# Output projection of a two-branch attention layer: 28 of 64 pairs of weight row tiles as seven block products of sums

## The chip, the cores and the metric

The kernel runs on one core of one Trainium2 chip. The metric is the device time in microseconds (us), the median of three runs; lower is better.

## What is computed

One decoder layer on 256 tokens (S) of 4096 channels (D), all in float32:

```python
proj = rmsnorm(x, g_pre) @ w_in          # 18336 columns, split into the parts below
o_a = causal_dense_attention(...) * silu(gate_a)      # branch A, 16 heads, 2048 wide
o_b = indexed_sparse_attention(...) * silu(gate_b)    # branch B, 16 heads, 2048 wide
merged = sigmoid(merge_a) * (o_a @ p_a) + sigmoid(merge_b) * (o_b @ p_b)
out = x + merged @ w_o                   # w_o is 4096 x 4096
```

The change concerns the last line, `merged @ w_o`, and what leads into it.

## The kernel before

Every float32 matrix product is made of three products of split operands: each operand is a high part (rounded to the type that TensorE takes at full rate) and a low part (the rest), and `mm3` issues high x high, low x high and high x low (L96, L97, L98) into one PSUM accumulator. The stationary side of a product is a 128 x 128 block of the transposed activations, the moving side 128 x 512 of a weight.

**The weight stream.** `run_streams` walks over a list, `plan`, of units. A unit is two weight row tiles (256 rows) by 512 columns: one DMA of 512 KB into `raw`, one cast on ScalarE (ACT) into `hi` (L218), one subtraction on VectorE (DVE) into `lo` (L226), and on TensorE (PE) 2 row tiles x 2 token tiles x 3 = 12 products of 128 x 512. `hi` and `lo` have three buffers and are issued two units ahead, `raw` has four and its DMA is issued six units ahead. All engines work through their instructions in the order in which the program issued them, each engine on its own. PE holds no instruction back for another engine except through semaphores.

**Background work.** All other work is written as generators. `tick`, called once per unit, lets them go on as far as a credit for DVE and ACT allows; `drain` runs them to their end at once. What a generator issues stands in the engines' order where it was issued.

**The last part.** For each of 8 chunks of 512 columns the stream has 16 units of `w_in` for each of the two sigmoid gates, 8 units of `p_a` and 8 of `p_b`; then `merged` (the tile `sa`, products and sums on DVE) is transposed on PE, and for chunks 0 to 6 stored to DRAM (`mt_d`). When the product with `p_a` of chunk 7 begins, `pre_last` starts seven background loads (`load_mt`): each reads one stored chunk into a tile `mts` (two buffers, DMA issued by GpSimd, POOL) and splits it, one ACT cast and one DVE subtraction of 128 x 1024, into `mh` and `ml` (tiles `h0`.., `l0`..), the stationary side of the output projection. Chunk 7 is transposed and split without going through DRAM. The projection itself is 8 chunks of 512 columns x 16 units of `w_o`, in the same stream; `final` adds `x` and stores.

Of the kernel before, what the change touches and what calls it, by code (L numbers as in the profile page):

```python
# [37 lines left out]
def kernel(ctx: ExitStack, tc: tile.TileContext, x, positions, g_pre, w_in, g_q_lat,  # L38
# [18 lines left out]
    class Meter:  # L57
        """An engine whose instructions are charged, by their size, to the background's share of its time."""
# [75 lines left out]
    def release(what):  # L134
        held[what] -= 1
# [40 lines left out]
    plan = []  # L176

# [9 lines left out]
    def run_streams():  # L187
# [43 lines left out]
        # the first pair of weight tiles is split tile by tile, on both engines, to start the products early  # L231
# [30 lines left out]
        for i, (spec, u) in enumerate(units):  # L262
            stat, w, segs, done, pre, each = spec
            if u == 0:
# [7 lines left out]
                if spec is units[-1][0]:  # L272
                    accs[id(spec)][0][1] = flat(ps_at.tile([P, 2, S], F32, name="at"))
# [8 lines left out]
            for kk in range(2):  # L282
# [14 lines left out]
                elif i == n - 1:  # L297
                    continue
                else:
                    for m in range(2):  # L300
                        ms = slice(m * P, (m + 1) * P)
                        mm3(accm[m][:, :wd], xh[:, ms], xl[:, ms], his[i][:, kk, :wd], los[i][:, kk, :wd],
                            k == 0, k == nk - 1)
# [4 lines left out]
            if i == n - 1:  # L308
                for m in range(2):
                    ms = slice(m * P, (m + 1) * P)  # L310
                    for kk in range(2):
                        k = 2 * u + kk
                        xh, xl = stat[1](k)
                        mm3(accm[m], xh[:, ms], xl[:, ms], his[i][:, kk, :], los[i][:, kk, :], False, kk == 1)
                    final_rows(accm[m], m)
                continue
            his[i] = los[i] = None
            if k == nk - 1:
                active.insert(0, done(acc))

# [1 line left out]
    # products of zeros keep the tensor engine busy until the first data is there, so that its clock is up by then  # L322
    zeros = cp.tile([P, 512], BF16, name="zeros")
# [9 lines left out]
    zero1 = cp.tile([P, 1], F32, name="zero1")  # L333
    dve.memset(zero1, 0.0)
    nhalf = cp.tile([P, 16], F32, name="nhalf")
    dve.memset(nhalf, -0.5)
    warm = cp.tile([P, 1], F32, name="warm")
# [7 lines left out]
    cst_sb = cp.tile([P, 33], F32, name="cst_sb")  # L345
    gT = cp.tile([P, 48], F32, name="gT")
    grot = cp.tile([P, 2, 64], F32, name="grot")
    posb = cp.tile([P, S], F32, name="posb")
    posp = cp.tile([P, 2], F32, name="posp")
    cm = cp.tile([P, 2, S], F32, name="cm")  # L350
    rope_q = cp.tile([P, 2, 2, 2, 64], F32, name="rope_q")
    rope_k = cp.tile([P, 2, 2, 64], F32, name="rope_k")
    r = cp.tile([P, 2], F32, name="r")
    krr = cp.tile([P, 2, 64], F32, name="krr")
    sskr = cp.tile([P, 2], F32, name="sskr")
    ssx = cp.tile([P, 2, 8], F32, name="ssx")
# [3 lines left out]
    wk_stack = ExitStack()  # L360
# [187 lines left out]
    def prep_rope():  # L548
# [21 lines left out]
        # rope_*[.., 0, ..]: multiplies x; rope_*[.., 1, ..]: multiplies x with its halves swapped  # L570
# [138 lines left out]
    def softmax_pv(s, nmx, sign, vh, vl, o_dst):  # L709
        """exp(sign * s + nmx), where nmx is minus the maximum of sign * s."""  # L710
# [310 lines left out]
    # each pair's two short streams lie within a long one, whose time its attention takes  # L1021
# [10 lines left out]
    M = {"go": [None, None], "mh": [], "ml": []}  # L1032

    def open_p():
        A["stack"].close()
        wk_stack.close()
        pp = M["pp"] = ctx.enter_context(tc.tile_pool(name="ppool", bufs=1))
        for br in range(2):
            M["go"][br] = (pp.tile([P, NH, S], F32R, name=f"goh{br}"), pp.tile([P, NH, S], F32R, name=f"gol{br}"))
# [42 lines left out]

    def load_mt(c):
# [5 lines left out]
        split(M["mh"][c], M["ml"][c], raw)  # L1089
# [6 lines left out]

    def done_pb(j):
        def done(acc):
            sa, sb = M["sa"], M["sb"]
            dve.tensor_tensor(sb, acc, sb, op=ALU.mult)  # L1100
            release("acc")
            dve.tensor_tensor(sa, sa, sb, op=ALU.add)
            if j < 7:
                spawn(store_merged(sa, j), ready=None)
                yield
            else:
                yield
                yield
                for kp in range(2):
                    tr = transpose_merged(sa, kp)  # L1110
                    split(flat(M["mh"][7][:, 2 * kp:2 * kp + 2, :]), flat(M["ml"][7][:, 2 * kp:2 * kp + 2, :]), tr)
                    yield
        return done

    def pre_last():
# [3 lines left out]
        for c in range(7):  # L1119
            spawn(load_mt(c), space=2)  # L1120

    for j in range(8):
# [4 lines left out]
        stream(stat_go(1), p_b, [(c0, 512)], done_pb(j))  # L1127

# [1 line left out]
    stat_m = (KT, lambda k: (M["mh"][k // 4][:, k % 4, :], M["ml"][k // 4][:, k % 4, :]))  # L1130

    def final(j):
        c0 = 512 * j

        def pre():
            xr = M["xr", j] = M["pp"].tile([P, 2, 512], F32, name="sb" if j % 2 else "xr")
            nc.gpsimd.dma_start(xr, xf[:, c0:c0 + 512].rearrange("(m p) c -> p m c", p=P))

        def done(acc):
            xr = M["xr", j]  # L1140
            dve.tensor_tensor(xr, acc, xr, op=ALU.add)
            release("acc")
            nc.gpsimd.dma_start(of[:, c0:c0 + 512].rearrange("(m p) c -> p m c", p=P), xr)
            yield

        stream(stat_m, w_o, [(c0, 512)], done, pre=pre)

    for j in range(8):
        final(j)

    def final_rows(acc, m):
        """The last chunk's rows of one token tile, in two halves so that the first is under way early."""
        xr = M["xr", 7]
        for q in range(2):
            cs = slice(256 * q, 256 * q + 256)
            dve.tensor_tensor(xr[:, m, cs], acc[:, cs], xr[:, m, cs], op=ALU.add)
            nc.sync.dma_start(of[m * P:(m + 1) * P, 7 * 512 + 256 * q:7 * 512 + 256 * q + 256], xr[:, m, cs])
# [3 lines left out]
    drain()  # L1161

# [42 lines left out]
```

## Time and profile before

| | |
|---|---|
| median of three runs | 2530.6 us (2530.31 to 2530.65) |
| span of the profiled execution, first to last instruction | 2528.1 us |
| PE busy | 2521.0 us (100% of the span) |
| DVE busy | 1392.0 us (55%) |
| ACT busy | 1221.6 us (48%) |
| POOL busy | 88.6 us (4%) |
| granted TensorE clock, mean | 1.000 |

The span leaves out what lies before the first and after the last instruction; against the median of the runs that is 2.5 us. A profiled PE matmul's own duration overlaps the next one's; its price is the distance from its start to the next start.

### The profile page before, as it was taken

What the parts mean: (1) busy time and instruction counts of PE and PEld (TensorE: products, weight loads), DVE (VectorE), ACT (ScalarE), POOL (GpSimd) and SP (SyncE); (2) the same over time, 40 slices, a digit from 0 to 9 for tenths busy, and PEclk for the clock granted to TensorE, in tenths of its full rate; (3) what the DMA queues carried; (4) which work ended last, traced back from release to release, by engine and by line L of the source; (5) the groups of instructions that cost most, each with busy time, mean ns of one, the idle gap of its engine ahead of it and who ended that gap; (6) DMA issues with size and microseconds to landing.
All of it is one profiled execution on the core that took longest, in us unless ns stands there. A gap on an engine that the chain in (4) does not pass through costs nothing.

```text
span 2528.1 us, 31510 instructions
## 1 busy us (share of the span) xinstructions
PE 2521.0 (100%) x12054; PEld 2108.7 (83%) x12054; DVE 1392.0 (55%) x1689; ACT 1221.6 (48%) x1646; POOL 88.6 (4%) x119
## 2 busy tenths in 40 slices
PE   9999999999999999999999999999999999999999
PEld 7988888888888888888888888888888888888887
DVE  5666696655666655655544444444444444644444
ACT  6555545555665555554444444444444434433333
POOL 2000000000000000000000000000000000000000
PEclk9999999999999999999999999999999999999999
DMA  7655565555555565557665656565656566666664
GB/s 245 185 168 166 160 187 161 167 183 175 181 185 177 186 183 186 185 179 244 214 199 195 197 196 198 194 198 193 199 192 200 192 216 205 237 226 214 217 217 158
DMA packets 259878, 490.46 MB, mean 194 GB/s; under 512 B 24660, under 2 KB 38096, under 8 KB 259728
## 3 DMA queue, kind: packets, MB, share of 16 engines
q1 hardware_dynamic: 251104, 460.38, 57.3%
q0 software_dynamic: 8576, 28.06, 3.2%
q8 instruction: 94, 1.54, 0.2%
q14 instruction: 56, 0.46, 0.0%
q10 hardware_dynamic: 48, 0.02, 0.0%
HBM read 474.24 MB, written 14.16 MB: 193 GB/s over the span
## 4 chain that ended last, share of the span: by engine, by line
PE 99%; DMA 0%; SPq 0%; issue 0%; DVE 0%; ACT 0%; DVEq 0%
PE acc L96 31%; PE acc L97 31%; PE acc L98 31%; PE tr L119 2%; PE at L96 1%; PE at L98 1%; PE at L97 1%; PE tr L618 0%; DMA raw<-in_w_in 0%; PE at L656 0%; PE at L657 0%; PE tr L826 0%; PE at L986 0%; PE at L987 0%; PE tr L925 0%
## 5 line engine op out<-in xcount | busy, mean ns | idle before, releaser
L226 DVE TENSOR_TENSOR lo<-raw,hi 128x1024 fp32r<-128x1024 f32 (+3 forms) x880 | 1064.4, 1210 | 1062.8 <-ACT hi L218 1053.3
L218 ACT CAST hi<-raw 128x1024 fp32r<-128x1024 f32 (+3 forms) x880 | 914.8, 1041 | 1054.9 <-PE acc L97 1004.5
L96 PE MATMUL acc<-hi,h 128*128 128x512 f32 (+1 forms) x2780 | 1091.8, 393 | 0.0
L97 PE MATMUL acc<-hi,l 128*128 128x512 f32 (+1 forms) x2780 | 1081.6, 389 | 0.8 <-DVE l L75 0.8
L98 PE MATMUL acc<-lo,h 128*128 128x512 f32 (+1 forms) x2780 | 1080.7, 389 | 0.0
L98 PEld LDWEIGHTS acc<-lo,h 128*128 128x128 f32 x2780 | 522.0, 188 | 109.3
L97 PEld LDWEIGHTS acc<-hi,l 128*128 128x128 f32 x2780 | 522.3, 188 | 101.5 <-DVE l L75 1.7
L96 PEld LDWEIGHTS acc<-hi,h 128*128 128x128 f32 x2780 | 522.1, 188 | 100.7
L96 PE MATMUL acc<-hi,goh 128*128 128x512 f32 x512 | 199.2, 389 | 0.0
L97 PE MATMUL acc<-hi,gol 128*128 128x512 f32 x512 | 199.2, 389 | 0.0
L98 PE MATMUL acc<-lo,goh 128*128 128x512 f32 x512 | 199.2, 389 | 0.0
L96 PEld LDWEIGHTS acc<-hi,goh 128*128 128x128 f32 x512 | 96.1, 188 | 20.0
L98 PEld LDWEIGHTS acc<-lo,goh 128*128 128x128 f32 x512 | 96.1, 188 | 20.0
L97 PEld LDWEIGHTS acc<-hi,gol 128*128 128x128 f32 x512 | 96.1, 188 | 19.9
L75 ACT ACTIVATE s<-s,nmx 128x256 f32<-128x256 f32 x64 | 32.1, 502 | 59.7 <-DVE nmx L75 59.7
L96 PE MATMUL acc<-hi,cqh 128*128 128x384 f32 x128 | 44.6, 349 | 0.0
L97 PE MATMUL acc<-hi,cql 128*128 128x384 f32 x128 | 43.3, 338 | 0.0
L98 PE MATMUL acc<-lo,cqh 128*128 128x384 f32 x128 | 43.2, 338 | 0.0
L75 ACT ACTIVATE nat<-acc,r 128x512 f32<-128x512 f32 (+1 forms) x70 | 42.4, 657 | 0.1
L1080 POOL DMA_DIRECT2D mt_d<-mts x7 | 3.7, 533 | 847.8 <-ACT mts L75 847.8
L75 ACT ACTIVATE s<-at 128x512 f32<-128x512 f32 x32 | 19.2, 600 | 27.7 <-PE at L657 27.6
L75 ACT CAST pth<-tr 128x512 fp32r<-128x512 f32 x32 | 18.8, 587 | 28.1 <-PE tr L119 28.1
(247 smaller groups left out, 1372.8 us busy)
## 6 DMA issues: line engine op xcount, KB each, us to landing
raw<-in_w_in SPq DMA_DIRECT2D x559, 512.0 KB, 3.5
raw<-in_w_o SPq DMA_DIRECT2D x128, 512.0 KB, 3.3
raw<-in_p_a SPq DMA_DIRECT2D x64, 512.0 KB, 3.3
raw<-in_p_b SPq DMA_DIRECT2D x64, 512.0 KB, 3.2
raw<-in_w_uq SPq DMA_DIRECT2D x32, 384.0 KB, 3.2
raw<-in_w_ukv SPq DMA_DIRECT2D x16, 512.0 KB, 3.7
raw<-in_w_in SPq DMA_DIRECT2D x18, 256.0 KB, 2.9
go_d<-go POOLq DMA_DIRECT2D x16, 256.0 KB, 4.1
```

The lines of the kernel that those rows point to most:

```text
L75: return fn(*args, **kw)
L96: nc.tensor.matmul(o, ah, bh, start=start, stop=False)
L97: nc.tensor.matmul(o, al, bh, start=False, stop=False)
L98: nc.tensor.matmul(o, ah, bl, start=False, stop=stop)
L119: nc.tensor.transpose(tr[:, a * S + m * P:a * S + (m + 1) * P], src_of(a, m), ident)
L218: nc.scalar.copy(t[:, ks, :width(i)], raws[i][:, ks, :width(i)])
L226: nc.vector.tensor_tensor(t[:, ks, :wd], raws[i][:, ks, :wd], his[i][:, ks, :wd].bitcast(F32), op=ALU.subtract)
L1080: nc.gpsimd.dma_start(mt_d[:, 4 * j:4 * j + 4, :], dst)
```

## The change

The output projection is taken out of the stream. It now goes over 4 blocks of 1024 columns; in each block, a step is one pair of weight row tiles (256 rows) by 1024 columns. A plain step (`unit_p`) is 8 block products of 128 x 128 by 128 x 512, that is 24 PE products. In a sum step (`unit_s`, pairs 0, 2, .. 12) the two token tiles, the two row tiles and the two column halves form a 2 x 2 by 2 x 2 block product, which is built from 7 products of sums and differences of blocks (the Winograd form of Strassen's scheme), that is 21 PE products. There are 28 sum steps and 36 plain ones. The sums of the weight blocks are made in each sum step on DVE (`prep_sums`), the sums of the activation blocks once per chunk (`split_mt`); the last additions are made once per block (`sums_early`, `sum_late`). Four PSUM accumulators hold the results `c` and four the sums `p1`, `p5`, `p6`, `p7`.

Pairs 1 and 3 of block 0 stay in the old stream as four units (`BRIDGE`), while the new tiles are opened. In the first of them all background work that is left is drained, the first three weight tiles of the new form are requested and the first sums are made; the merge of chunk 7 is issued behind that unit, its transposes behind the second, its split behind the third. `x` is added by accumulating DMAs of POOL.

```diff
+    def split_mt(c, raw):
+        sh, sl, mh, ml = M["sh"][c], M["sl"][c], M["mh"][c], M["ml"][c]
+        split(mh[:, 2:4, :], ml[:, 2:4, :], raw[:, 2:4, :])
+        split(sh[:, 0, :], sl[:, 0, :], raw[:, 0, :P])
+        split(flat(sh[:, 1:3, :]), flat(sl[:, 1:3, :]), raw[:, 1, :])
+        a11, a21, a12, a22 = raw[:, 0, :P], raw[:, 0, P:], raw[:, 1, :P], raw[:, 1, P:]
+        dve.tensor_tensor(a22, a21, a22, op=ALU.add)
+        dve.tensor_tensor(a21, a21, a11, op=ALU.subtract)
+        dve.tensor_tensor(a11, a22, a11, op=ALU.subtract)
+        dve.tensor_tensor(a12, a12, a11, op=ALU.subtract)
+        split(mh[:, 0:2, :], ml[:, 0:2, :], raw[:, 0:2, :])
+
     def load_mt(c):
...
-        split(M["mh"][c], M["ml"][c], raw)
+        split_mt(c, raw)
...
+    def bridge_first():
+
+        go_stack.close()
+        open_banks()
...
+        for i in range(3):
+            raw_dma(i)
+        prep_sums(0)
+
+    def bridge_acc(h):
+        def get():
+            if h == 0:
+                drain()
+                bridge_first()
+            return [F["c"][0, h], F["c"][1, h]], None
+        return get
...
+    bridge_hooks.extend((last_merge, last_transpose, last_split, lambda: None))
+
+    order0 = "s0 p5 s2 p7 s4 p9 s6 p11 s8 s10 p13 s12 p14 p15".split()
...
+    def prep_sums(i):
...
+        v(t[:, 0:2, :], raw[:, 3, None, :].to_broadcast([P, 2, 512]), raw[:, 1:3, :], op=ALU.subtract)
+        v(t[:, 2, :], raw[:, 1, :], t[:, 1, :], op=ALU.subtract)
+        v(raw[:, 3, :], raw[:, 0, :], t[:, 2, :], op=ALU.subtract)
+
+    def prep(i):
...
+        prep_sums(i)
+        raw = raws[i]
+        n = 3 if units[i][1] == "s" else 4
+        h = his[i] = F["pb"].tile([P, 4, 512], F32R, name="whi", bufs=3)
+        nc.scalar.copy(h[:, :n, :], raw[:, :n, :])
+        if n == 3:
+            t = tops[i]
+            ht = hits[i] = F["pa"].tile([P, 4, 512], F32R, name="whs", bufs=2)
+            nc.scalar.copy(ht[:, 0:3, :], t)
+            nc.scalar.copy(ht[:, 3, :], raw[:, 3, :])
+        l = los[i] = F["pb"].tile([P, 4, 512], F32R, name="wlo", bufs=3)
+        nc.vector.tensor_tensor(l[:, :n, :], raw[:, :n, :], h[:, :n, :].bitcast(F32), op=ALU.subtract)
+        if n == 3:
+            lt = lots[i] = F["pa"].tile([P, 4, 512], F32R, name="wls", bufs=2)
+            nc.vector.tensor_tensor(lt[:, 0:3, :], t, ht[:, 0:3, :].bitcast(F32), op=ALU.subtract)
+            nc.vector.tensor_tensor(lt[:, 3, :], raw[:, 3, :], ht[:, 3, :].bitcast(F32), op=ALU.subtract)
...
+        product(F["p5"], mh[:, s1], ml[:, s1], th[:, 1, :], tl[:, 1, :], p == 12)
...
+        product(cc[1, 0], ph[:, 2, :], pl[:, 2, :], th[:, 3, :], tl[:, 3, :])
...
+    def run_blocks():
+        st_stack.close()
...
+        open_sums()
+        prep(0)
+        prep(1)
+        for i, (b, kind, p) in enumerate(units):
...
+            raw_dma(i + 2)
+            prep(i + 2)
+            raw_dma(i + 3)
+            if kind == "s":
+                unit_s(i, p)
+                if p == 12:
+                    sums_early()
...
+            if last and b < 3:
+                for q in QUARTERS:
+                    sum_late(*q)
+                for q in QUARTERS:
+                    add_x(b, *q)
```

In the following rows a number at the end of a name is that of the buffer. DVE before, where the stream passes from `p_b` to `w_o`: `lo_17545`, `lo_17565`, `lo_17586` are the first three units of `w_o`, `sb`, `sa` the merge of chunk 7, `l7` its split.

```order
L226 TENSOR_TENSOR lo_17545<-raw_17467,hi_17543 128x1024
L75 TENSOR_TENSOR l6_17256<-mts_17517,h6_17255 128x1024
L226 TENSOR_TENSOR lo_17565<-raw_17487,hi_17563 128x1024
L226 TENSOR_TENSOR lo_17586<-raw_17507,hi_17584 128x1024
L75 TENSOR_TENSOR sb_17272<-acc_17421,sb_17272 128x1024
L75 TENSOR_TENSOR sa_16964<-sa_16964,sb_17272 128x1024
L226 TENSOR_TENSOR lo_17606<-raw_17529,hi_17604 128x1024
L226 TENSOR_TENSOR lo_17624<-raw_17547,hi_17622 128x1024
L75 TENSOR_TENSOR l7_17258<-tr_17634,h7_17257 128x512
```

DVE now, from the second bridge unit (`lo_17631`) to the third (`lo_17694`) and the merge; `mts_17621` and `mts_17639` are the loaded chunks 5 and 6, `wsum` the first weight sums.

```order
L231 TENSOR_TENSOR lo_17631<-raw_17537,hi_17629 128x1024
L78 TENSOR_TENSOR l5_17264<-mts_17621,h5_17263 128x512
...
L78 TENSOR_TENSOR l6_17266<-mts_17639,h6_17265 128x512
L78 TENSOR_TENSOR sl6_17282<-mts_17639,sh6_17281 128x128
L78 TENSOR_TENSOR sl6_17282<-mts_17639,sh6_17281 128x256
L78 TENSOR_TENSOR mts_17639<-mts_17639 128x128 x4
L78 TENSOR_TENSOR l6_17266<-mts_17639,h6_17265 128x512
L1242 TENSOR_TENSOR wsum_17688<-wraw_17679 128x1024
L1243 TENSOR_TENSOR wsum_17688<-wraw_17679,wsum_17688 128x512
L1244 TENSOR_TENSOR wraw_17679<-wraw_17679,wsum_17688 128x512
L231 TENSOR_TENSOR lo_17694<-raw_17567,hi_17692 128x1024
L78 TENSOR_TENSOR sb_17296<-acc_17473,sb_17296 128x1024
L78 TENSOR_TENSOR sa_16974<-sa_16974,sb_17296 128x1024
```

Between the second bridge unit's `lo` and the third's stand now the splits of chunks 5 and 6 and the first weight sums, and the merge stands behind them.

PE now, at the end of the second bridge unit (`lo_17631`): the transposes of `sa`, then the third unit.

```order
L99 MATMUL at_17675<-hi_17629,h0_17253 128x512
L100 MATMUL at_17675<-hi_17629,l0_17254 128x512
L101 MATMUL at_17675<-lo_17631,h0_17253 128x512
L1205 MATMUL acc_17726<-ident_90,sa_16974 128x128 x8
L99 MATMUL tr_17672<-hi_17692,h1_17255 128x512
```

Before, the eight transposes stood four and four inside the third and the fourth unit of `w_o`; now all eight stand in front of the third.

ACT now, from the split of chunk 7 on to the first step of the blocks, with the engines and DMA queues that each row waits for in brackets:

```order
L78 CAST h7_17267<-mts_17735 128x1024 [waits Activation_49]
L1253 CAST whi_17771<-wraw_17679 128x1536 [waits DMAHW0_49,DMAHW7_49,DVE_49,PE_49]
L1257 CAST whs_17773<-wsum_17688 128x1536
L1258 CAST whs_17773<-wraw_17679 128x512
L1253 CAST whi_17781<-wraw_17682 128x2048 [waits DMAHW2_49,DMAHW1_49,Activation_49]
```

The first cast of the blocks, `whi_17771`, takes memory that `run_blocks` frees by closing the stream's pool, and its wait for PE is for the last product of the fourth bridge unit. Before, no cast of `w_o` waited for more than the unit three before it.

## Rows read from the trace of the kernel before

**Rows 1.** The page: busy time by engine; then the chain that ended last.

```profile
PE 2521.0 (100%) x12054; PEld 2108.7 (83%) x12054; DVE 1392.0 (55%) x1689; ACT 1221.6 (48%) x1646; POOL 88.6 (4%) x119
...
PE 99%; DMA 0%; SPq 0%; issue 0%; DVE 0%; ACT 0%; DVEq 0%
```

**Rows 2.** Busy time by stretch, clock, DMA: chunk 7's p_a and p_b; output projection.

```profile
2131.60:2175.10 43.50, 43.50 (x193) 36.04 (x192) 28.58 (x24) 24.68 (x25) 3.37 (x6) 1.00 0.77 266
2175.10:2524.50 349.40, 349.34 (x1545) 288.88 (x1543) 166.70 (x140) 134.10 (x128) 10.02 (x14) 1.00 0.59 206
```

**Rows 3.** Timeline where w_o begins, all engines: start us, duration us, engine, line, operation.

```profile
2174.91 0.39 PE L98 MATMUL acc<-lo,goh 128*128 128x512 f32 x1
2175.11 1.05 ACT L218 CAST hi<-raw 128x1024 fp32r<-128x1024 f32 x1 [1.67 <-PE acc L97]
2175.13 0.39 PE L96 MATMUL acc<-hi,h 128*128 128x512 f32 x1
2175.36 0.39 PE L97 MATMUL acc<-hi,l 128*128 128x512 f32 x1
2175.59 0.39 PE L98 MATMUL acc<-lo,h 128*128 128x512 f32 x1
2176.19 1.23 DVE L226 TENSOR_TENSOR lo<-raw,hi 128x1024 fp32r<-128x1024 f32 x1 [1.50 <-ACT hi L218]
2177.34 1.22 DVE L75 TENSOR_TENSOR sb<-acc,sb 128x1024 f32<-128x1024 f32 x1
2178.59 1.23 DVE L75 TENSOR_TENSOR sa<-sa,sb 128x1024 f32<-128x1024 f32 x1
2179.73 1.22 DVE L226 TENSOR_TENSOR lo<-raw,hi 128x1024 fp32r<-128x1024 f32 x1
```

**Rows 4.** Groups by line and form on DVE and ACT: count, busy us, mean ns.

```profile
L75 DVE TENSOR_TENSOR vl<-nat,vh 128x512 fp32r<-128x512 f32 x8 | 5.5, 683 | 0.0
L75 DVE TENSOR_TENSOR ropetmp<-nat,rope_q 128x128 f32<-128x128 f32 x16 | 3.9, 283 | 0.0
L75 DVE TENSOR_TENSOR vbl<-go,vbh 128x256 fp32r<-128x256 f32 x1 | 0.4, 425 | 0.1
L75 ACT CAST vh<-nat 128x512 fp32r<-128x512 f32 x8 | 4.9, 618 | 0.0
```

**Rows 5.** The tile mts: times from DMA issue to landing; page's issues of w_o and mts.

```profile
DMA to landing us min/median/max: 3.9/5.0/7.7
...
raw<-in_w_o SPq DMA_DIRECT2D x128, 512.0 KB, 3.3
mts<-mt_d POOLq DMA_DIRECT2D x7, 512.0 KB, 4.7
```

**Rows 6.** Timeline of PE at the kernel's start, and the first 4 us by engine.

```profile
1.20 2.31 PE L329 MATMUL at<-zeros 128*128 128x512 bf16 x5 [1.20 <-DVE nhalf L75]
3.65 1.08 PE L119 MATMUL tr<-ident,nat 128*128 128x128 f32 x4
5.81 0.93 PE L288 MATMUL acc<-hi,h 128*128 128x512 f32 x1
6.65 0.50 PE L289 MATMUL acc<-hi,l 128*128 128x512 f32 x1
6.99 0.40 PE L288 MATMUL acc<-hi,h 128*128 128x512 f32 x1
7.46 0.60 PE L119 MATMUL tr<-ident,nat 128*128 128x128 f32 x4
11.18 0.63 PE L119 MATMUL tr<-ident,nat 128*128 128x128 f32 x4 [1.28 <-DMA nat<-in_x]
...
0.00:4.00 4.00, 2.66 (x7) 0.96 (x8) 0.30 (x3) 1.49 (x2) 3.41 (x12) 1.00 0.50 152
```

**Rows 7.** Timeline of the end of the kernel.

```profile
2523.61 2.12 SPq L1157 DMA_DIRECT2D out<-sb  x4
2524.05 0.39 PE L98 MATMUL at<-lo,h 128*128 128x512 f32 x1
2524.48 0.76 DVE L75 TENSOR_TENSOR sb<-at,sb 128x256 f32<-128x256 f32 x2 [0.60 <-PE at L98]
```

More of the change, by code (lines that the diff above doesn't have):

```diff
@@ L176 @@
     plan = []
+    BRIDGE = (1, 3)
+    bridge, bridge_hooks = {}, deque()
     def stream(stat, w, segs, done, pre=None, each=None, now=True):
@@ L263, in run_streams @@
             stat, w, segs, done, pre, each = spec
-            if u == 0:
+            if id(spec) in bridge:
+                if id(spec) not in accs:
+                    accs[id(spec)] = bridge[id(spec)]()
+            elif u == 0:
                 if pre is not None:
@@ L296, in run_streams @@
                         nc.tensor.matmul(accm[m][:, :wd], xh[:, ms], los[0][:, kk, :wd], start=False, stop=False)
-                elif i == n - 1:
-                    continue
                 else:
+                    first = 2 * BRIDGE[0] if id(spec) in bridge else 0
                     for m in range(2):
@@ L307, in run_streams @@
                     tick((0.95 * (6 * wd / 1200 - 0.07 - wd / 480), 0.95 * (6 * wd / 1200 - 0.2 - wd / 700)))
[L308 to L316, printed above, removed]
             his[i] = los[i] = None
-            if k == nk - 1:
+            if id(spec) in bridge:
+                if bridge_hooks:
+                    bridge_hooks.popleft()()
+            elif k == nk - 1:
                 active.insert(0, done(acc))
-    zeros = cp.tile([P, 512], BF16, name="zeros")
+    zeros = cq.tile([P, 512], BF16, name="zeros")
     nc.vector.memset(zeros, 0.0)
@@ L1095, in done_pa, with merge @@
         yield
+    def merge(acc):
+        sa, sb = M["sa"], M["sb"]
+        dve.tensor_tensor(sb, acc, sb, op=ALU.mult)
+        release("acc")
+        dve.tensor_tensor(sa, sa, sb, op=ALU.add)
+        return sa
     def done_pb(j):
         def done(acc):
[L1099 to L1112, printed above, removed]
+            sa = merge(acc)
+            spawn(store_merged(sa, j), ready=None)
+            yield
         return done
@@ L1119, in pre_last, with done_last @@
         for c in range(7):
+            M["sh"].append(M["sx"].tile([P, 3, P], F32R, name=f"sh{c}"))
+            M["sl"].append(M["sx"].tile([P, 3, P], F32R, name=f"sl{c}"))
             spawn(load_mt(c), space=2)
+    def done_last(acc):
+        M["acc"] = acc
+        while len(active) > 1 or pending:
+            yield
     for j in range(8):
@@ L1126 @@
         stream(stat_go(0), p_a, [(c0, 512)], done_pa, pre=pre_last if j == 7 else None)
-        stream(stat_go(1), p_b, [(c0, 512)], done_pb(j))
+        stream(stat_go(1), p_b, [(c0, 512)], done_pb(j) if j < 7 else done_last)
     stat_m = (KT, lambda k: (M["mh"][k // 4][:, k % 4, :], M["ml"][k // 4][:, k % 4, :]))
[L1132 to L1157, printed above, removed]
+    F = {}
+    def open_banks():
+        tr = [bank() for _ in range(2)]
+        at = [flat(ps_at.tile([P, 2, S], F32, name="at")) for _ in range(2)]
+        F["c"] = {(0, 0): tr[0], (0, 1): tr[1], (1, 0): at[0], (1, 1): at[1]}
+        F["on"] = set()
@@ new lines, in open_sums, with product @@
+    def open_sums():
+        t = [ps_acc.tile([P, 2, 512], F32, name="acc") for _ in range(2)]
+        F["p1"], F["p7"], F["p5"], F["p6"] = t[0][:, 0], t[0][:, 1], t[1][:, 0], t[1][:, 1]
+    def product(o, ah, al, bh, bl, stop=False):
+        new = id(o) not in F["on"]
+        F["on"].add(id(o))
+        mm3(o, ah, al, bh, bl, new, stop)
+    def bridge_first():
+        go_stack.close()
+        open_banks()
+        c = F["c"]
+        F["on"].update(id(v) for v in c.values())
+        F["pa"] = ctx.enter_context(tc.tile_pool(name="wide", bufs=1))
+        for i in range(3):
+            raw_dma(i)
+        prep_sums(0)
@@ new lines, in bridge_acc, with last_merge @@
+    def bridge_acc(h):
[5 more added lines that the diff above has]
+        return get
+    for p in BRIDGE:
+        for h in range(2):
+            if p == BRIDGE[0]:
+                spec = (stat_m, w_o, [(512 * h, 512)], None, None, None)
+                bridge[id(spec)] = bridge_acc(h)
+                F["spec", h] = spec
+            plan.append((F["spec", h], p))
+    def last_merge():
+        M["sa"] = merge(M["acc"])
@@ new lines, in last_transpose @@
+    def last_transpose():
+        tr = ps_acc.tile([P, 2, 512], F32, name="acc")
+        mg = M["sa"]
+        for kp in range(2):
+            for a in range(2):
+                for m in range(2):
+                    nc.tensor.transpose(tr[:, kp, a * S + m * P:a * S + (m + 1) * P],
+                                        mg[:, m, (kp * 2 + a) * P:(kp * 2 + a + 1) * P], ident)
+        dst = M["pp"].tile([P, 4, S], F32, name="mts", bufs=2)
+        for kp in range(2):
+            act.copy(flat(dst[:, 2 * kp:2 * kp + 2, :]), tr[:, kp])
+        M["raw7"] = dst
@@ new lines, in last_split, with raw_dma @@
+    def last_split():
+        split(M["mh"][7], M["ml"][7], M["raw7"])
+        small_stack.close()
+    bridge_hooks.extend((last_merge, last_transpose, last_split, lambda: None))
+    order0 = "s0 p5 s2 p7 s4 p9 s6 p11 s8 s10 p13 s12 p14 p15".split()
+    units = [(0, u[0], int(u[1:])) for u in order0]
+    for b in range(1, 4):
+        units += [(b, "p" if p % 2 or p == 14 else "s", p) for p in range(16)]
+    raws, tops, his, los, hits, lots = {}, {}, {}, {}, {}, {}
+    def raw_dma(i):
+        if i >= len(units) or i in raws:
+            return
+        b, kind, p = units[i]
+        t = raws[i] = F["pa"].tile([P, 4, 512], F32, name="wraw", bufs=3)
+        for kk in range(2):
+            q = 1 - kk if kind == "s" else kk
+            row = (2 * p + kk) * P
+            nc.sync.dma_start(flat(t[:, 2 * q:2 * q + 2, :]), w_o[row:row + P, 1024 * b:1024 * b + 1024])
@@ new lines, in unit_p @@
+    def unit_p(i, p, after=None):
+        for m in range(2):
+            for h in range(2):
+                for kk in range(2):
+                    k = 2 * p + kk
+                    ah, al = stat_m[1](k)
+                    ms = slice(m * P, (m + 1) * P)
+                    product(F["c"][m, h], ah[:, ms], al[:, ms], his[i][:, 2 * kk + h, :], los[i][:, 2 * kk + h, :],
+                            p == 15 and kk == 1)
+                if after is not None:
+                    after(m, h)
@@ L1161 @@
     drain()
+    run_blocks()
 def _constants():
```

104 lines of the change are left out of this document (82 added, 22 removed).

## The prediction

> **What bounds the kernel now.** I read the page first. PE is busy for the whole span and 99% of the chain that ended last is PE, while DVE and ACT are busy for half of it [rows 1]. So a product that is taken out of PE is time won, and a wait put into PE is time lost. The busy time by stretch shows the same for the output projection alone: 349.4 us in which PE has no gap and DVE works for 166.7 and ACT for 134.1; in the 43.5 us before it, where chunk 7 meets `p_a` and `p_b`, DVE is at 28.6 and ACT at 24.7 of 43.5 [rows 2]. The timeline at the seam gives the prices. Two PE products start 0.227 us apart (2175.13, 2175.36, 2175.59), which makes 2.72 us for a unit of 12 and 348.2 us for 1536, the stretch less the transposes. A cast starts as its unit's buffer comes free, the subtraction 1.08 us later, so `lo` is ready 2.3 us into a lead of 5.4. A DVE instruction of 128 x 1024 takes 1.23 us; the next independent one starts after 1.15, one that needs its result after 1.25 [rows 3].
>
> **What the change removes.** 28 sum steps of 21 products in place of 24 are 84 products less; at 0.2267 us that is **-19.0 us**. A plain step stays at 5.44 us, a sum step is 4.76.
>
> **What it adds inside the blocks.** From DVE's rows at 512 and 1024 elements [rows 3, 4] an element costs about 1.05 ns and an instruction 0.15 us, so 128 x 1536 is about 1.76 us and 128 x 2048 about 2.3 (estimates from those rows). A sum step has on DVE 1024 + 2 x 512 for the sums, then 1536, 1536, 512: 6.8 us end to end, some 6.4 with the overlap of starts; a plain step 2.3. A pair of steps is 9.1 of DVE's time at most, against 10.2 us of PE. ACT has about 3.6 and 1.9. Weight bytes per second rise by 7% in a sum step's pair of steps, from a DMA share of 0.59 [rows 2], and a weight tile is requested three steps ahead against 3.3 us to land [rows 5]. Walked through with the semaphores' order (cast when the step three before has ended, sums, two subtractions), a sum step's operands are ready 2 to 5 us before PE wants them, about 1 us in the third step of block 0. At a block's end DVE adds 2.8 us for `sums_early`, with plain steps behind it, and 2.7 for `sum_late`; the next block starts with four products into other accumulators (2.7 us), which covers the release of the first result bank. So I take **0** inside the blocks: the 1.1 us that PE has over DVE in each pair hides it. If DVE needed 12% more than I reckon, that cover would be gone (a rival below). The end is alike: one last quarter, two additions of 256 columns, two DMAs [rows 7]; the accumulating loads of `x` have 10 us before they are wanted.
>
> **What it adds at the seam.** This is the costly part. A chunk's split, formerly one cast and one subtraction of 1024, is now a chain across two engines: DVE 512, 128, 256, then four dependent ones of 128, an ACT cast of 512, a DVE subtraction of 512. With 683, 283 and 425 ns on DVE and 618 on ACT [rows 4], less 0.08 where starts overlap and plus 0.03 to 0.06 where they depend: 0.60 + 0.20 + 0.45 + 4 x 0.31 + 0.06 + 0.62 + 0.03 + 0.60 = 3.8 us until DVE is free, and the next unit's cast stands behind the cast of 512 on ACT. The splits of chunks 0 to 4 stand two units apart or more. Two units with a split are 2 x 1.15 + 3.8 = 6.1 us for 5.4 us of PE: the lead of 3 us shrinks but holds, because four units lie between the splits of chunks 2 and 3.
>
> I put time 0 at the fourth unit of chunk 7's `p_b` product; the bridge units then start at 13.6, 16.3, 19.0 and 21.8. DVE, in the order that the change section shows: `lo` of the sixth unit until 2.4, split 3 until 6.2, two `lo` (their casts waited for split 3) until 8.8, split 4 until 12.6, `lo` of bridge units one and two until 15.3, split 5 until 19.1, split 6 until 22.9, the three instructions of the first weight sums 2.6 us until 25.5, `lo` of the third bridge unit until 26.6, the two of the merge until 29.1. The transposes need the merge and stand on PE in front of the third bridge unit, which could have started at 19.0. So PE, in order, waits from 19.0 to 29.1: **+10.1 us**. Before, the merge had ended 4.7 us after `w_o` began [rows 3]. Bounds: 8 if the casts never hold a split up; 12.6 if chunk 6's load is late. Its issue waits for split 4 (12.6), and it is wanted at 18.5; with 4.7 us to land and POOL's half microsecond it makes it, with the 7.7 of the slowest one [rows 5] it comes 2.5 late.
>
> The second wait is at the fourth bridge unit's end. The first cast of the blocks waits for that unit's last product, since its memory is the stream's. Then 1536 on ACT (1.5 us, from 618 ns at 512 and 1.05 us at 1024 [rows 3, 4]), again 1536 for the sums (1.45), upon which PE does two products; the third needs the subtraction of 1536, which follows on DVE behind another of 1536 (1.5 + 1.75 + 1.75 = 5.0 from the start, less 0.45 for the two products): **+4.5 us**. Bounds 3.0 (the two casts alone) and 6.
>
> **The clock after the gap.** At the kernel's start, after idle, five products of 512 columns take 2.31 us, 0.46 each instead of 0.227; four transposes take 1.08 us, later 0.60; the close spacing is there from 6.65 us on, 5.4 us after the first product. That is the lower of the two levels, 1.2 GHz, though the granted clock of that stretch reads 1.00. An idle of 1.28 us before 11.18 brought no slow transposes (0.63) [rows 6]. A gap of 10 us is nearer to the start's idle than to 1.28 us, so I let PE run at half rate for as long as at the start, and half of 5.4 us is lost: **+2.7 us**. Bounds 0 (no fall) and 5.4 (again after the second gap).
>
> The Trainium skill, "TensorE: Matmul & The Clock Gate", section "HAM oscillation — how this bites in real kernels", says that a gap in PE's work sends the clock back to 1.2 GHz and that the warm-up is then paid again. By that rule the term is in the sum and the time is the forecast; without it the time is the first rival's. Apart from the start no run here shows it.
>
> **The sum.** On the profiled span of 2528.1: -19.0 + 10.1 + 4.5 + 2.7 = -1.7, so 2526.4; the median of the runs lies 2.5 us above the span, so **2528.9 us**. I take 0.2% (5 us) as what a measurement of this kernel tells from no change: forecast "same".
>
> **Rivals.**
> (a) The clock does not fall: -4.4, 2526.2 us. For it: the column of granted clock. Against it: the start's spacing. With the waits at their lower bounds it becomes -8, 2522.6.
> (b) The bridge covers the seam, as four units (10.9 us) would if DVE reached the merge early; then only the second wait remains: 2530.6 - 19.0 + 4.5 = 2516.1 us. Against it: DVE's order puts two splits of 3.8 and sums of 2.6 ahead of the merge, and DVE leaves no order.
> (c) Slower: DVE becomes the bound inside the blocks. It decides from 10.2 us of DVE per pair of steps, 1.1 more than I reckon; each half microsecond beyond costs 28 x 0.5 = 14 us, so some 2543 us. For it: instructions of 1536 and sums that reach across a step do not occur before, and waits between ACT and DVE in one step are serial. Against it: the rows at 512 and 1024 lie on one line.
> (d) The seam is worse: load of chunk 6 late (+2.5), second wait 6 (+1.5), clock down twice (+2.7): 2535.6 us.
>
> **How the numbers follow.** Forecast 0.58 (2525.5 to 2532); (a) 0.15, of which a third beyond 5 us faster; (b) 0.07; (c) 0.12; (d) 0.08, half of it beyond 5 us slower. The rest of the forecast's spread goes 0.05 to faster and 0.02 to slower. Faster 0.07 + 0.05 + 0.05 = 0.17; slower 0.12 + 0.04 + 0.02 = 0.18; same 0.65. The range takes in (a) with its lower waits and (d), and leaves out most of (b) and (c): 2522.5 to 2536.
>
> **What the new profile would show.** Spacing of 0.227 us in the blocks and 1452 products in the projection: the first term. A PE gap of about 10 us in front of eight transposes, put down to DVE's `sa`: the second; none there would be (b). A gap of 3 us and one of 1.5 at the first sum step, put down to ACT's `whs` and DVE's `wls`: the third. Transposes at 1.1 us for four and products 0.43 apart after the gap: the fourth; at 0.227 it is (a). Idle PE in front of every sum step, with DVE near 100%, is (c). The forecast is wrong if PE's idle at the seam is far from 15 us or the blocks have gaps of their own.

## The result, and the profile after

The changed kernel takes **2549.4 us** (median of 4 runs, 2548.3 to 2551.7) against 2530.5 us before on the same chip: ratio 1.0077, 95% interval 1.0063 to 1.0092. It is slower by 19 us, outside the range, where no measurable change was forecast. The profiled span went from 2528.1 to 2548.1 us.

The page after, beside [rows 1]; busy time by engine, and the chain that ended last:

```profile
PE 2527.6 (99%) x11970; PEld 2097.8 (82%) x11970; DVE 1523.4 (60%) x1837; ACT 1254.1 (49%) x1666; POOL 98.9 (4%) x132
...
PE 98%; DVE 1%; DMA 0%; issue 0%; ACT 0%; SPq 0%; DVEq 0%
```

There are 84 products fewer, as the diff says, and yet PE is busy for 6.6 us more. So a product must take longer on average. First the parts that were forecast. All that PE waited for from 2150 us on:

```profile
PE acc L1205 <- DVE sa L78: 9.7, 1, 9.7
PE acc L99 <- ACT whs L1257: 2.9, 1, 2.9
PE acc L101 <- DVE wls L1263: 0.9, 1, 0.9
```

These are the three waits of the prediction, at their places and nearly at their sizes, and there is no other one, inside the blocks or at their ends. The timeline of DVE shows the chain that was counted, ending in the merge (`sa`) for which PE waits; [rows 3] have the merge of before:

```profile
2192.10 1.29 DVE L78 TENSOR_TENSOR l<-mts,h 128x512 fp32r<-128x512 f32 x2 [0.69 <-ACT h L78]
...
2195.92 0.69 DVE L78 TENSOR_TENSOR l<-mts,h 128x512 fp32r<-128x512 f32 x1 [0.68 <-ACT h L78]
2196.53 1.22 DVE L1242 TENSOR_TENSOR wsum<-wraw 128x1024 f32<-128x1024 f32 x1
...
2199.12 1.22 DVE L231 TENSOR_TENSOR lo<-raw,hi 128x1024 fp32r<-128x1024 f32 x1
2200.25 1.22 DVE L78 TENSOR_TENSOR sb<-acc,sb 128x1024 f32<-128x1024 f32 x1
2201.50 1.22 DVE L78 TENSOR_TENSOR sa<-sa,sb 128x1024 f32<-128x1024 f32 x1
```

The timeline of PE, behind the first wait and behind the other two:

```profile
2202.87 1.94 PE L1205 MATMUL acc<-ident,sa 128*128 128x128 f32 x8 [9.68 <-DVE sa L78]
2204.47 0.78 PE L99 MATMUL tr<-hi,h 128*128 128x512 f32 x1
...
2206.74 0.60 PE L101 MATMUL at<-lo,h 128*128 128x512 f32 x1
2207.17 0.41 PE L99 MATMUL tr<-hi,h 128*128 128x512 f32 x1
...
2216.50 0.80 PE L101 MATMUL acc<-wls,h 128*128 128x512 f32 x1 [0.87 <-DVE wls L1263]
2217.09 0.63 PE L99 MATMUL acc<-whs,h 128*128 128x512 f32 x1
2217.51 0.63 PE L100 MATMUL acc<-whs,l 128*128 128x512 f32 x1
...
2220.89 0.40 PE L99 MATMUL tr<-whi,sh 128*128 128x512 f32 x1
```

Products 0.43 us apart are products at the lower clock, 1.2 GHz. They stand behind the 9.7 us of idle and once more behind 2.9 and 0.9 us of it. The granted clock shows both stretches (busy time by window: PE, PEld, DVE, ACT, POOL, then PEclk, DMA share, GB/s):

```profile
1500.00:1530.00 30.00, 30.00 (x133) 24.62 (x132) 16.89 (x14) 11.31 (x12) 0.00 (x0) 1.00 0.64 190
...
2195.00:2215.00 20.00, 9.19 (x34) 7.46 (x34) 11.29 (x12) 8.12 (x10) 0.00 (x0) 0.72 0.18 71
2215.00:2250.00 35.00, 34.13 (x138) 27.18 (x137) 33.02 (x27) 18.02 (x14) 0.00 (x0) 0.92 0.64 220
```

That PE's clock falls back behind a gap and that the warm-up is paid again is what the Trainium skill, "TensorE: Matmul & The Clock Gate", section "HAM oscillation — how this bites in real kernels", says, and behind the 9.7 us the trace agrees.

What was not forecast is in the first of these rows, 670 us ahead of the change: 133 products in 30 us, at a granted clock of 1.00. The same window before (transposes and shorter products count too, so the number alone isn't a spacing):

```profile
1500.00:1530.00 30.00, 30.00 (x136) 24.83 (x135) 15.36 (x14) 12.19 (x12) 0.00 (x0) 1.00 0.62 190
```

The timeline of PE there, after, shows 0.69 us from one L99 to the next, where [rows 3] show 0.227 us for each product, 0.680 for three:

```profile
1500.38 0.39 PE L99 MATMUL acc<-hi,goh 128*128 128x512 f32 x1
1500.62 0.39 PE L100 MATMUL acc<-hi,gol 128*128 128x512 f32 x1
1500.84 0.39 PE L101 MATMUL acc<-lo,goh 128*128 128x512 f32 x1
1501.07 0.39 PE L99 MATMUL acc<-hi,goh 128*128 128x512 f32 x1
```

Averaged over the start times of 1140 to 2190 us, the three are 0.232, 0.226 and 0.229 us, 0.687 together. The first product with `w_o` starts at 2187.52 us after and at 2175.13 before [rows 3]: **12.4 us are lost ahead of the seam**, in work whose instructions are the same. In the blocks it is more:

```profile
2280.00:2510.00 230.00, 230.00 (x991) 186.50 (x990) 198.60 (x167) 113.81 (x86) 17.43 (x24) 1.00 0.71 226
```

230 / 991 = 0.2321 us for a product; over some 1400 products of the blocks, 5.4 ns more for each than 0.2267 are 7.6 us. The account of the span: 2528.1 + 12.4 (ahead of the seam) - 19.0 (84 products) + 13.5 (three waits) + 4.5 (clock: 2.1 and 2.4, from the rows above, against 0.84 us for eight transposes as in h2 below and 0.227 for a product) + 7.6 (blocks) = 2547.1, of 2548.1.

### The profile page after: what moved, and what is told of

It reads as the page before. It is cut to its first block, busy times and chain, and to the rows that moved or that the text cites. A ratio compares the mean times of both kernels' runs of the same rounds, so it can differ in the third digit from the quotient of the medians.

```text
span 2548.1 us, 31501 instructions
## 1 busy us (share of the span) xinstructions
PE 2527.6 (99%) x11970; PEld 2097.8 (82%) x11970; DVE 1523.4 (60%) x1837; ACT 1254.1 (49%) x1666; POOL 98.9 (4%) x132
## 4 chain that ended last, share of the span: by engine, by line
PE 98%; DVE 1%; DMA 0%; issue 0%; ACT 0%; SPq 0%; DVEq 0%
PE acc L99 28%; PE acc L101 28%; PE acc L100 27%; PE at L99 2%; PE at L101 2%; PE at L100 2%; PE tr L99 2%; PE tr L101 2%; PE tr L100 2%; PE tr L122 2%; PE tr L616 0%; DMA raw<-in_w_in 0%; PE at L654 0%; PE at L655 0%; PE tr L824 0%
## 5 line engine op out<-in xcount | busy, mean ns | idle before, releaser
L231 DVE TENSOR_TENSOR lo<-raw,hi 128x1024 fp32r<-128x1024 f32 (+3 forms) x756 | 912.6, 1208 | 888.1 <-ACT hi L223 877.2
L223 ACT CAST hi<-raw 128x1024 fp32r<-128x1024 f32 (+3 forms) x756 | 780.3, 1034 | 849.0 <-PE acc L100 819.0
L99 PE MATMUL acc<-hi,h 128*128 128x512 f32 (+1 forms) x2300 | 909.6, 395 | 0.6 <-ACT h L78 0.6
L101 PE MATMUL acc<-lo,h 128*128 128x512 f32 (+1 forms) x2300 | 899.5, 391 | 0.0
L100 PE MATMUL acc<-hi,l 128*128 128x512 f32 (+1 forms) x2300 | 895.0, 389 | 0.9 <-DVE l L78 0.8
L101 PEld LDWEIGHTS acc<-lo,h 128*128 128x128 f32 x2300 | 432.0, 188 | 95.1
L100 PEld LDWEIGHTS acc<-hi,l 128*128 128x128 f32 x2300 | 432.4, 188 | 87.2 <-DVE l L78 1.7
L99 PEld LDWEIGHTS acc<-hi,h 128*128 128x128 f32 x2300 | 432.5, 188 | 81.8 <-ACT h L78 1.1
L99 PE MATMUL acc<-hi,goh 128*128 128x512 f32 x512 | 201.7, 394 | 0.0
L1253 ACT CAST whi<-wraw 128x2048 fp32r<-128x2048 f32 (+1 forms) x62 | 106.1, 1712 | 139.4 <-PE at L100 95.8
L1260 DVE TENSOR_TENSOR wlo<-wraw,whi 128x2048 fp32r<-128x2048 f32 (+1 forms) x62 | 127.0, 2048 | 46.8 <-ACT whi L1253 46.7
L101 PEld LDWEIGHTS acc<-lo,goh 128*128 128x128 f32 x512 | 96.1, 188 | 22.6 <-DVE lo L231 0.2
L99 PEld LDWEIGHTS acc<-hi,goh 128*128 128x128 f32 x512 | 96.3, 188 | 19.2
L99 PE MATMUL tr<-whi,h 128*128 128x512 f32 x164 | 65.0, 396 | 0.0
L99 PE MATMUL at<-whi,h 128*128 128x512 f32 x136 | 54.0, 397 | 0.0
```

The lines of the kernel that those rows point to most:

```text
L99: nc.tensor.matmul(o, ah, bh, start=start, stop=False)
L100: nc.tensor.matmul(o, al, bh, start=False, stop=False)
L101: nc.tensor.matmul(o, ah, bl, start=False, stop=stop)
L223: nc.scalar.copy(t[:, ks, :width(i)], raws[i][:, ks, :width(i)])
L231: nc.vector.tensor_tensor(t[:, ks, :wd], raws[i][:, ks, :wd], his[i][:, ks, :wd].bitcast(F32), op=ALU.subtract)
L1253: nc.scalar.copy(h[:, :n, :], raw[:, :n, :])
```

## The experiments

All against the kernel before on the same chip: 2530.1 to 2530.5 us in each comparison.

What could make the same products slower? The diff has lines that the front left out, since they change no instruction: the stream's tiles went to the other end of SBUF, and small tiles to a pool that is opened behind the big ones.

```diff
-    st = ctx.enter_context(tc.tile_pool(name="stream", bufs=1))
     big = ctx.enter_context(tc.tile_pool(name="big", bufs=1))
+    st = st_stack.enter_context(tc.tile_pool(name="stream", bufs=1, side="right"))
+    cq = wk_stack.enter_context(tc.tile_pool(name="consts2", bufs=1))
```

In the compiled programs `raw`, `hi`, `lo` and the stationary tiles (`h`, `l`, `goh`, `gol`) start a multiple of 4096 bytes apart before. In the changed kernel all of them start at 32 modulo 64, and the stationary ones lie 192 bytes, modulo 256, from `hi` and `lo`. Three theories were set up: A, the start address itself; B, the place far up in SBUF; C, the denser work of the blocks.

**e1_after_64.** The changed kernel with three pads of 32 bytes; the tiles of the stream, of the stationary side and of the blocks all start at the same place modulo 256.

```diff
+    right = ctx.enter_context(tc.tile_pool(name="right", bufs=1, side="right"))
+    right.tile([P, 8], F32, name="pad_r")
+    big.tile([P, 8], F32, name="pad_l")
...
+    cq.tile([P, 8], F32, name="pad_q")
```

> The changed kernel with three pads of 32 bytes, so that the big tiles start at SBUF addresses divisible by 64, as they did before the change; the changed kernel has them at 32 past such an address. Nothing else differs. Theory A (the start address of tiles slows PE's products and the DMAs): the 20.6 us by which the products' spacing had grown are gone, the waits at the seam stay: about 2529 us. Theory B (the stream's tiles lie far up in SBUF, on the other side, and that slows them): unchanged, 2549 us. Theory C (the denser work of the blocks slows PE): the part ahead of the seam stays slow too, so unchanged.

Measured: 2526.7 us, ratio 0.9985 (0.9975 to 0.9994), 22.6 us less than without the pads and 2.3 less than theory A said (a part of that is explained at the end). The windows in which the changed kernel has 133 and 991 products:

```profile
1500.00:1530.00 30.00, 30.00 (x138) 24.84 (x137) 15.75 (x13) 11.90 (x14) 0.41 (x1) 1.00 0.67 191
2280.00:2510.00 230.00, 230.00 (x1017) 190.53 (x1016) 197.97 (x163) 116.72 (x88) 17.39 (x24) 1.00 0.71 227
```

The stream still lies at the far end and the blocks are as dense, so B and C fall: moving the tiles, by 32 bytes each, is worth the whole loss. The waits stay:

```profile
PE acc L1209 <- DVE sa L81: 9.7, 1, 9.7
PE acc L102 <- ACT whs L1261: 2.9, 1, 2.9
PE acc L104 <- DVE wls L1267: 1.4, 1, 1.4
```

**e2_before_32, e3_before_32_stream, e4_before_32_rest.** The kernel before, with pads of 32 bytes: ahead of everything (e2); ahead of the stream's tiles and again behind them (e3); behind them alone (e4).

```diff
+    cp.tile([P, 8], F32, name="pad_c")     # e2
+    st.tile([P, 8], F32, name="pad_s")     # e3
+    big.tile([P, 8], F32, name="pad_b")    # e3, e4
```

> The kernel before with one pad of 32 bytes ahead of all tiles: all of them start 32 bytes past where they were, no instruction differs. Theory A: slower, by 0.5 to 0.9 per cent, 2543 to 2553 us. Theory B and C: unchanged, 2530.5 us.

> The kernel before with only the stream's tiles (raw, hi, lo) 32 bytes past an address divisible by 64; all other tiles keep such addresses. Theory A says nothing on which tiles matter: if it is the moving side of the products and the DMAs' targets, this has all of the second kernel's loss (2543 to 2553 us); if it is the stationary side, 2530.5. Theory B and C: 2530.5 us.

> The kernel before with the stream's tiles kept and all tiles behind them (the stationary sides h, l, goh, gol and the background's) 32 bytes further. Theory A: the complement of the third kernel; if the stationary side matters, all of the loss is here (2543 to 2553 us), else 2530.5. Theory B and C: 2530.5 us.

Measured: e2 2530.2 us (0.9998, 0.9989 to 1.0008), e3 2585.9 (1.0217, 1.0200 to 1.0235), e4 2584.9 (1.0214, 1.0198 to 1.0229). In e2 all tiles start at 32 modulo 64, as in the changed kernel, and nothing happens: theory A falls. In e3 and e4 the stationary tiles lie 32 bytes from a multiple of 4096 behind the stream's, at different absolute places, and the price is the same, 55 us, more than any of the three theories had. So it is the **distance** between them (theory D). Edits of one and two lines that leave each instruction as it was make the kernel 2.1 to 2.2% slower.

**g1_before_64_rest, g2_before_128_rest, g5_before_256_rest, g6_before_192_rest.** As e4, with 64, 128, 256 and 192 bytes.

```diff
+    big.tile([P, 16], F32, name="pad_b")   # g1; 32 in g2, 64 in g5, 48 in g6
```

> The kernel before, with 64 bytes left free between the stream's tiles and all the others. Theory D (a product's price is set by where the tile that PE streams past lies relative to the tile that it loads, start address against start address; in the changed kernel they lay 64 bytes apart, modulo 128): the triple of products goes from 0.680 to about 0.687 us as in the changed kernel's stream, some 20 to 27 us over the kernel, so 2550 to 2557 us, less than half of what 32 bytes gave (2585). Rival E (any shift between the stream and the rest costs the same, since it only stops a fortunate lockstep): 2585 us. Rival F (only offsets within 64 bytes count, and the changed kernel has its slow products for another reason): 2530 us.

> The same with 128 bytes left free. Theory D with offsets counted modulo 128: 2530 us, no change. Theory D with offsets counted modulo 256 or more (the version of the changed kernel with three pads, which was fast, had 256 modulo 512): between 2531 and 2557 us. Rival E: 2585 us. Rival F: 2530 us.

> The kernel before, with 256 bytes left free between the stream's tiles and all the others (32, 64 and 128 bytes gave 2585, 2585 and 2580 us). If the distance counts modulo 256 bytes, as the kernel with the three pads lets one think (its distances leave no rest by 256 and its products take 0.227 us): 2530 us, within 0.2%. If any distance that is no multiple of 4096 (or of 512) costs: 2565 to 2590 us.

> The kernel before, with 192 bytes left free between the stream's tiles and all the others: the same distance, modulo 256, as between the stream's tiles and the stationary ones in the changed kernel. If that distance alone makes the changed kernel's slow products: the triple of products 0.687 us instead of 0.680 in the stream, as there, which over the whole kernel is 20 to 28 us, so 2550 to 2558 us. If the distance costs what 32, 64 and 128 bytes cost: 2580 to 2586 us, and the changed kernel's smaller price has another reason. If it costs nothing: 2530 us, and the distance is not what slows the changed kernel.

Measured; the last column is the mean distance from the start of one 128 x 512 product to the next, from 2300 to 2500 us of each trace:

| distance, bytes | kernel | median, us | ratio (95%) | spacing, us |
|---|---|---|---|---|
| 0 | e2 | 2530.2 | 0.9998 (0.9989 to 1.0008) | 0.2267 |
| 32 | e4 | 2584.9 | 1.0214 (1.0198 to 1.0229) | 0.2333 |
| 64 | g1 | 2585.0 | 1.0214 (1.0196 to 1.0233) | 0.2333 |
| 128 | g2 | 2580.0 | 1.0193 (1.0177 to 1.0209) | 0.2333 |
| 192 | g6 | 2545.5 | 1.0060 (1.0043 to 1.0077) | 0.2289 |
| 256 | g5 | 2530.2 | 0.9998 (0.9988 to 1.0007) | 0.2267 |

The distance counts modulo 256: 0 and 256 cost nothing, and no other value tried is free. For g1 I expected the changed kernel's own price, 2550 to 2557, and was wrong: 64 and 192 are not alike. Alone, g1 spoke for rival E, any shift at one price, and against F; g5 and g6 refute E. For g6 I expected 2550 to 2558; it is 2545.5, but the pattern is the one looked for. Its timeline of PE, in the projection:

```profile
2300.33 0.39 PE L97 MATMUL acc<-hi,h 128*128 128x512 f32 x1
2300.56 0.39 PE L98 MATMUL acc<-hi,l 128*128 128x512 f32 x1
2300.79 0.39 PE L99 MATMUL acc<-lo,h 128*128 128x512 f32 x1
2301.02 0.39 PE L97 MATMUL acc<-hi,h 128*128 128x512 f32 x1
```

Averaged, 0.232, 0.226 and 0.229 us, the changed kernel's three numbers to the nanosecond. And its last `p_b` product starts at 2185.92 us against 2174.91 before [rows 3], 11.0 us of the changed kernel's 12.4. My estimate was too high because it took the dearer triple for the whole kernel: between 20 and 1140 us, with the attention's work between them, products are 0.2289 us apart on average in the kernel before too and 0.2293 in g6, so the 192 bytes add little there.

**g3_before_32_raw, g4_before_32_hi.** Which two tiles? In g3 only `raw`, which DMAs write and ACT and DVE read, lies off; in g4 `raw` and `hi` do, and `lo` does not.

```diff
+        st.tile([P, 8], F32, name="pad_s")   # g3: here; g4: behind the next line
         h0 = his[0] = st.tile([P, 2, 512], F32R, name="hi", bufs=LOOK_SPLIT + 1)
```

> The kernel before, with 32 bytes left free between raw and hi: only raw, which the weight DMAs write and which ACT and DVE read, lies 32 bytes off; hi, lo and the stationary tiles keep their distances. Theory D (it is PE's own two reads): 2530 us, within 0.2%. Rival G (it is the writes by DMA, or ACT and DVE reading raw, that meet PE's reads, or the DMA's own pace): up to 2585 us.

> The kernel before, with 32 bytes left free between hi and lo: hi (and raw) lie 32 bytes off the stationary tiles, lo does not. Two products of three stream hi, one streams lo. Theory D with each product paying for its own streamed tile: two thirds of 55 us, so about 2567 us, with the products that stream hi some 7 ns dearer than the one that streams lo. If the price hangs on hi alone or on the change from hi to lo: 2585 us. Rival G: 2530 us, since raw and hi keep their distance.

Measured: g3 2529.3 us (0.9997, 0.9988 to 1.0007); g4 2587.1 (1.0221, 1.0204 to 1.0237). So it isn't the DMAs, or ACT and DVE reading `raw`. Nor is it ACT and DVE writing `hi` and `lo`: in e4's trace, from 1600 to 1900 us, 98 products run while ACT, DVE and POOL are all idle, and they are 0.235 us apart. What is left is the tile that PE streams against the one that it loads. But the price isn't each product's own. In g4's timeline of PE:

```profile
1500.06 0.40 PE L98 MATMUL acc<-lo,h 128*128 128x512 f32 x1
1500.29 0.40 PE L96 MATMUL acc<-hi,h 128*128 128x512 f32 x1
1500.53 0.40 PE L97 MATMUL acc<-hi,l 128*128 128x512 f32 x1
1500.76 0.40 PE L98 MATMUL acc<-lo,h 128*128 128x512 f32 x1
```

the three take 0.70 us, and the product that streams `lo`, which lies right, is nearly as dear as the others (averaged from 1600 to 1900 us: 0.232 us against 0.234 and 0.235). I had expected 2567 us, two thirds of the price.

**h2_fill_gaps.** e1 with products, whose results are overwritten, in the two gaps.

```diff
+        for q in range(40):
+            nc.tensor.matmul(tr[:, q % 2], M["mh"][0][:, 0, :P], flat(M["mh"][0][:, 0:2, :]), start=True, stop=True)
         for kp in range(2):
             for a in range(2):
...
+        for q in range(12):
+            nc.tensor.matmul(F["p5"], M["mh"][0][:, 0, :P], flat(M["mh"][0][:, 0:2, :]), start=True, stop=True)
         prep(0)
```

> The changed kernel with the three pads, with 40 products of 128 x 512 put in front of the transposes of chunk 7 and 12 in front of the first step of the blocks; their results are overwritten. They take 9.1 and 2.7 us at 0.2267 us each, a little less than the waits there (9.7 and 4.3 us in two pieces). Theory K (the products at 0.43 us are the clock's fall after PE's idle): transposes 0.11 us and products 0.227 us apart all through the seam, 1.5 + 2.4 us less, so about 2523 us (2522 to 2525). Rival (products are slow there for another reason, such as the DVE and ACT work at the seam, or the twelve products come in the way of the first step): 2526 to 2529 us.

Measured: 2522.8 us, ratio 0.9970 (0.9958 to 0.9981). Its timeline of PE:

```profile
2187.45 1.09 PE L1211 MATMUL acc<-ident,sa 128*128 128x128 f32 x8 [0.55 <-DVE sa L81]
2188.29 0.48 PE L102 MATMUL tr<-hi,h 128*128 128x512 f32 x1
2188.61 0.40 PE L103 MATMUL tr<-hi,l 128*128 128x512 f32 x1
2188.85 0.40 PE L104 MATMUL tr<-lo,h 128*128 128x512 f32 x1
...
2199.07 0.55 PE L104 MATMUL acc<-wls,h 128*128 128x512 f32 x1 [1.35 <-DVE wls L1269]
2199.41 0.63 PE L102 MATMUL acc<-whs,h 128*128 128x512 f32 x1
2199.84 0.63 PE L103 MATMUL acc<-whs,l 128*128 128x512 f32 x1
```

Without the first gap, the eight transposes and the products behind them run at full rate (granted clock 1.00 from 2187 to 2192 us): the slow ones were the clock's. The second half failed: 1.35 us of waiting for `wls` are not covered by the twelve products, and behind them the slow products are back (granted clock 0.66 from 2199 to 2204 us). From the last `p_b` product to the end of the span it is 350.6 us here and 352.0 in e1: 1.4 us, the first fall's price alone (its products and transposes lose 1.5 in e1). The rest of the difference in the medians lies ahead of the seam and is not the filling's.

**h1_seam_early.** e1 with another order at the seam. All of the computation is done.

```diff
-    BRIDGE = (1, 3)
+    BRIDGE = (1, 3, 5, 7)
...
             raw_dma(i)
-        prep_sums(0)
+        last_merge()
...
-    bridge_hooks.extend((last_merge, last_transpose, last_split, lambda: None))
+    bridge_hooks.extend((lambda: split_a(5, M["raw", 5]), hook2, lambda: split_a(6, M["raw", 6]), hook4,
+                         lambda: None, hook6, lambda: prep_top(0), lambda: None))
-    order0 = "s0 p5 s2 p7 s4 p9 s6 p11 s8 s10 p13 s12 p14 p15".split()
+    order0 = "s0 p9 s2 p11 s4 p13 s6 p14 s8 s10 s12 p15".split()
```

(`split_a` is a split up to its four additions, `split_b` the rest; `hook2` is the transposes and `split_b` of chunk 5, `hook4` `split_b` of chunk 6 and the copy of chunk 7, `hook6` the first weight sums and the split of chunk 7, `prep_top` the casts and subtractions of these sums. Also in the edit: chunks 5 and 6 are loaded without being split in the background, and in the first sum step one block product stands earlier on PE.)

> The changed kernel with the three pads (2526.7 us there), with another order at the seam: the merge of chunk 7 is issued at the head of the bridge, the bridge has eight units (pairs 1, 3, 5, 7), the splits of chunks 5 and 6 stand in it in two halves each, and the casts and subtractions of the first step's weight sums stand ahead of the bridge's end. All of the computation is done. Theory S (the seam's cost is the order on DVE): in the kernel with the pads PE idles 9.7 + 2.9 + 1.4 = 14.0 us at the seam and the products at 0.43 us after each gap lose about 1.5 and 2.4 us more; about 2 us of it stay, at the first step, so some 2511 us (2507 to 2515), no gap over 1 us ahead of the transposes and no products at 0.43. Rival W (DVE has too much work there whatever the order, so that the wait only moves to the first step of the blocks): 2517 to 2527 us, with one gap of 4 us or more at the first step.

Measured: **2513.0 us**, ratio 0.9929 (0.9912 to 0.9945). What PE waits for from 1800 us on, and the transposes in the timeline:

```profile
PE tr L102 <- DVE ev L1353: 1.0, 1, 1.0
PE acc L104 <- DVE wls L1281: 1.0, 1, 1.0
PE tr L102 <- ACT hi L226: 1.0, 1, 1.0
PE tr L104 <- DVE lo L234: 0.5, 1, 0.5
```

```profile
2177.92 1.03 PE L1218 MATMUL acc<-ident,sa 128*128 128x128 f32 x8
```

Of 14.0 us of waiting at the seam 2.5 stay (the first of the four is at a block's end), and no product stands at 0.43. From the last `p_b` product to the end it is 339.4 us, against 352.0 in e1 and 353.2 before. DVE had no less to do (busy for 1521.7 us, 1522.6 in e1); what it did first was wrong. The bridge of twice the length, the halved splits and the earlier merge were changed together, so what each is worth isn't shown. This version beats both kernels.

## Why the prediction was wrong

**The step that failed** is "What the change removes", where it says that 84 products at 0.2267 us go and that a plain step stays at 5.44 us. The 0.2267 us of [rows 3] was taken for the price of a product; it is the price at a distance of 0 modulo 256. The change sets 192, the products cost 0.229 us in the stream and 0.232 in the blocks, and 20 us come on top, 12.4 of them in work that it doesn't touch. The working had no term for that, and no rival: the pools' lines were left out as if they moved nothing. e1 takes the 20 us away with the distance alone, and g6 makes 11.0 of the stream's 12.4 us in the kernel before.

The other steps, on the kernel with the right distance (e1), from the last `p_b` product to the end: 352.0 us against 353.2 before, -1.2 where the sum said -1.7. That the two are so near is in part luck: smaller waits (14.0 us for 14.6) and a dearer clock (some 3.5 for 2.7) cancel.

- **-19.0.** Borne out in size: 1017 products in 230 us are 0.2262 us each.
- **0 inside the blocks.** Right as it was meant, for waits: there is none. What the blocks lose is in the price of a product.
- **The first wait, +10.1.** 9.7, at its place and put down to `sa`. The DVE chain was counted right, and h1 shows that another order takes it away.
- **The second wait, +4.5.** 2.9 and 0.9 (2.9 and 1.4 in e1).
- **The clock, +2.7.** The mechanism is right (h2), the term was mis-sized: it fell twice, for 2.1 and 2.4 us (some 1.5 and 2.0 in e1). The fall after the second gap was only in the upper bound.
- **Rival (c), DVE as the bound in the blocks,** gives the changed kernel's time to some 6 us for a reason that is not there: PE has no wait in the blocks, and DVE's row of 1536 elements measures 1.75 us where 1.76 was estimated.

## What to carry to other kernels

A product's spacing in a trace is a price at one layout of SBUF: when a change moves pools, opens tiles in another order or adds a small tile ahead of large ones, compare the start addresses of what PE loads and what it streams; here a multiple of 256 bytes between them was the layout without a price. If the same instructions are dearer ahead of the place that a change touches, look at what it changes for the whole program. A wait at a seam is read from the order on the engine that is waited for: another order there was worth 12.6 us, two thirds of what the saved products bring.

## What the runs showed of the hardware

At full clock, in the projection, a 128 x 512 product is 0.2267 us, 544 cycles of 2.4 GHz, when the loaded and the streamed tile start a multiple of 256 bytes apart, and 0.2333 us, 560 cycles, at 32, 64 and 128 bytes; 192 bytes give 0.229. The Trainium skill, "TensorE: Matmul & The Clock Gate", section "Step-by-step: what each phase is for", says that PE has two independent SBUF read ports and that loading the next weights takes no read bandwidth from the running matmul; the runs differ: where the two tiles lie is worth up to 16 cycles in 544. That it is PE's two reads that meet is what is left when the writers are ruled out; no run shows it directly.

The kernel before pays a little of the same price. Its `ckh`, `ckl`, `cqh` and `cql`, the stationary tiles of the products with `w_ukv` and `w_uq` in branch A, start 128 bytes, modulo 256, from `hi` and `lo` in the compiled program; with the three pads (e1, h1, h2) they start at 0. The 192 products with `ckh` and `ckl` go from 0.232 to 0.227 us apart, and with those of `cqh` and `cql` that is 1.5 us of the 2 to 3 us by which e1, h1 and h2 reach the seam ahead of the kernel before, whose last `p_b` product starts at 2174.91 us (2172.88 in e1).

What stays open: why 192 costs about a third of 64; why a product that lies right becomes dear among others (g4's `lo`, and the changed kernel's sum steps, whose `whs` and `wls` lie at distance 0 and are still streamed at 0.231 us on average); where in the memory the two reads meet; and the rest, 0.5 us in e1 and some 1.3 and 1.6 in h1 and h2, of the lead at the seam. That filling alone prevents the second fall of the clock isn't shown; h1, which has no wait there over 1.0 us, doesn't have the fall.
